# One inference step of a streaming encoder layer on one core: a later product with the values, an earlier weight split, low parts and copies on other engines

## The chip, the core and the metric

The kernel runs on 1 core of one Trainium2 chip. The engines of a core run side by side, each working through its own instructions in the order of the program, and they wait for each other at semaphores. In the profile they are called PE (TensorE: matrix products and transposes), PEld (the loading of PE's weights), DVE (VectorE), ACT (ScalarE), POOL (GpSimd) and SP (SyncE, which here issues most of the DMAs; "SPq" marks a DMA that it issues). The metric is the device time of one execution in microseconds (us). Products read SBUF and write PSUM; POOL works on SBUF alone.

## The reference: what is computed

One layer of a two-branch attention block, in float32, for a prompt of 1024 new positions and for a sample of 64 positions that has 512 cached positions behind it. Each of the two goes through the same steps, cut down here:

```python
h = rms_norm(x, norm_w) @ w_in          # 1024 -> 6144 columns
sb_q, sb_k, sb_v, sb_z, cb_q, cb_k, cb_v, cb_z, g_sb, g_cb = split(h)
# branch A ("sb"), 8 heads of 64: stick-breaking attention
z = sb_q @ sb_k.T * 0.125
w = where(s < t, exp(log_sigmoid(z) + sum of log_sigmoid(-z) over s < j < t), 0)
o_sb = w @ sb_v
# branch B ("cb"), 8 heads of 64: softmax over a band of the last 8 chunks of 64 and the own one,
# q and k normalised per head, with a learned bias by relative position
o_cb = softmax(cb_q @ cb_k.T * 0.125 + bias) @ cb_v
b_sb = (o_sb * silu(sb_z)) @ w_proj_sb
b_cb = (o_cb * silu(cb_z)) @ w_proj_cb
y = x + (sigmoid(g_sb) * b_sb + sigmoid(g_cb) * b_cb) @ w_out
```

The outputs are `y` for prompt and sample, and the new keys and values of both branches.

## The kernel before

**Split numbers.** A float32 factor of the large projections is held as two parts: the high part is a rounded copy (made by ACT), the low part is the rest (the factor less its high part, made by DVE or POOL). Three products, high times high, high times low and low times high, are summed in PSUM. So each block of weights, when it has landed in `wraw`, is "split": `W.split` (line 127) issues a copy on ACT (`whi`, line 117) and a subtraction (`wlo`, line 124) on POOL, or on DVE if that is passed as the engine. Both have two buffers.

**Stages.** First come the projections of all columns (lines 453 to 697, up to some 523 us), whose results go to DRAM. Then comes attention (547 to some 822 us): branch A, then branch B, each in four pairs of heads, each pair with the sample's block first (t = 8, both heads in one block of 128 rows) and then eight blocks of 128 prompt positions for each of its two heads, 17 blocks for a pair. Last come branch A's output projection (`proj_sb`), branch B's (`proj_cb`, line 967) and the output matrix (line 1509).

**Attention step by step.** The loop at line 1262 goes through the 136 blocks in the order of `seq`; in step i it issues the work of several blocks at different stages:
- `qk(i)`: PE's scores of block i into `z` (three PSUM buffers); for branch A ACT turns them into sigmoids `be` (line 1100), for branch B DVE adds the bias (line 1102).
- `mid(i-1)` for branch A: DVE's scan over `be` (line 1119). For branch B `soft(i-1)` takes the exponential on ACT (line 1110), and `mid(i-2)` a reciprocal on DVE (line 1121) and a scaling on ACT (line 1122).
- `tr(i-4)`: PE transposes the block's weights, in groups of up to four 128 x 128 blocks, into `pt` (two PSUM buffers, line 1150); a copy takes each group to `wT` in SBUF, on ACT (line 1159) for branch A and every fourth of branch B, else on DVE (line 1161). The last 64 rows of the sample's block are a group of their own (line 1155).
- `av(...)`: when both heads of two blocks (or the sample's block) are transposed, the product of values and `wT` is due two steps later: `avq` holds it with its step. It goes to `o`, which has a single PSUM buffer, and DVE multiplies it with the gate (line 1198 or 1200); POOL then issues its store to `d_osb` or `d_ocb`.
- `fill(n)`: n products of other work, taken from the generator `run_fill`, so that PE has something to do between. In a step with m of them, m // 2 come ahead of `av` and `tr`, the others behind. How many a step gets is written out by hand in `early` (line 1254): 11 for the very first block, 7 for each of the two after it, and a share by width of what is left.

**What the fill products are.** First four "units", blocks of 128 columns of the last projection: for each of three ranges of positions (`ci`) 24 products, 72 for a unit (line 842). Units 0 and 1 run ahead of attention, unit 2 within branch A from its first step on, and unit 3 from step 75 on. Within a unit, at the first product of `ci` 1 (line 849), the load of the block after next is issued and the next block is split (line 854; on DVE until step 75). Then follows `proj_sb`: 12 rounds of 24 products, after each 12 of which DVE multiplies the accumulator with a gate and writes it to SBUF (line 952). The accumulators (`acc`) have two PSUM buffers.

**The end of attention.** When the loop is done, 61 products of `proj_sb` are left. Line 1376 interleaves them with the preparation of branch B's output `o`: for each range of positions, `load_og` (line 899) issues four loads from `d_ocb` into `ot` (two buffers, each for two pairs of heads), then some fill products follow, then `make_og`: for each pair the high part on ACT (line 904) and the low part (line 909) on POOL for even pairs, on DVE for odd ones, and all on POOL in the second range. Loads of gates (`load_gcb`) and of the output matrix (`wsum`, line 1388) follow on SP, and then twelve rounds of `proj_cb`, with the split of their next weights on POOL every third round, and the sums of output weights (line 1399, 1401) and the low parts of kept columns (line 1018) also on POOL.

Of the kernel before, what the change touches and what calls it, by code (L numbers as in the profile page):

```python
# [32 lines left out]
def hybrid_step_kernel(ctx: ExitStack, tc: tile.TileContext, x_prompt, x_sample, c_sbk, c_sbv, c_cbk, c_cbv,  # L33
# [3 lines left out]
    V, A, G, TE, SP = nc.vector, nc.scalar, nc.gpsimd, nc.tensor, nc.sync  # L37
# [105 lines left out]
    def xk(s, k):  # L143
        return xhl[s][k // 4][:, k % 4]
# [9 lines left out]
    units = [("ev_act", 5120 + 128 * j, (AF.Copy, d_g["cb"][j])) for j in range(4, KT)]  # L154
# [392 lines left out]
    with ExitStack() as ph:  # L547
# [104 lines left out]
        for i in range(len(pairs)):  # L652
            bank, s1, u2, u3 = {}, {}, {}, {}
            for s in range(7):
                n = 7 * i + s
# [179 lines left out]
    def run_fill():  # L835
        for j, (kind, c, args) in enumerate(units):
            wh, wl = W.sp.pop(("u", j))
            for ci, (a, b) in enumerate(CH):
                ps = psF.tile([128, 512], F32, name="acc")
                for k in range(KT):  # L840
                    for n, (w, x) in enumerate(((wh, 0), (wh, 1), (wl, 0))):
                        TE.matmul(ps[:, :b - a], w[:, k], xk(x, k)[:, a:b], start=k == 0 and n == 0,  # L842
                                  stop=k == KT - 1 and n == 2)
                        if ci == k == n == 0 and j + 1 == len(units):
                            load_og("sb", 0, late["y"])
                            late["tbx"] = ExitStack()
                            late["tbp"] = late["tbx"].enter_context(tc.tile_pool(name="tbp", bufs=1, side="right"))
                            load_gate(late["tbp"], "gt", 0, d_g["sb"][0:2], 0)
                        if ci == 1 and k == 0 and n == 0:
                            if j + 2 < len(units):  # L850
                                load_unit(j + 2)
                            else:
                                load_proj(j + 2 - len(units))
                            W.split(("u", j + 1) if j + 1 < len(units) else ("p", 0), None if "sb" in late else V)
                        if k == KT - 1 and n == 2:
                            KIND[kind](*args, ci, a, b, ps)
                            if ci == 2:
                                prog[0] = j
                            if j + 1 == len(units):
                                ogq.extend((f, ci, p) for p in range(NPAIR) for f in (og_hi, og_lo))  # L860
                        yield 1
                        og_step(n == 0)
        late["tbt"] = xpool.tile([128, KT, T], F32, name="xm")
        for i, v in enumerate(proj_sb(late["tbp"])):
            yield v
            og_step(i % 3 == 2)
# [3 lines left out]
    def og(b, s, p):  # L870
        return xhl[s][s][:, p] if b == "sb" else late["og"][s][:, p]
# [4 lines left out]
    def load_proj(i):  # L876
        if i < 8:
            w = w_proj_sb if i < 4 else w_proj_cb
            c = (i % 4) * 256
            if i < 4:  # L880
                W.load(("p", i), wpool, w[:, c:c + 256].rearrange("(k p) n -> p k n", p=128), [128, 4, 256])
                return
            raw = wpool.tile([128, 4, 256], F32, name="wraw")
            for g in range(2):
                n = 512 * g + 128 * (i - 4)
                SP.dma_start(raw[:, :, 128 * g:128 * g + 128], w[:, n:n + 128].rearrange("(k p) n -> p k n", p=128))
            W.raw["p", i] = (raw, wpool, [128, 4, 256], "")
# [18 lines left out]
    def og_lo(b, ci, p):  # L906
        a, e = CH[ci]
        ot = ots.pop((ci, p))
        (V if p % 2 and (b, ci) != ("cb", 1) else G).tensor_tensor(out=og(b, 1, p)[:, a:e], in0=ot[:, :e - a],
                                          in1=og(b, 0, p)[:, a:e].bitcast(F32), op=OP.subtract)  # L910

    def make_og(b, ci):
# [6 lines left out]
    def load_gate(pool, name, key, us, ci):  # L919
        a, e = CH[ci]  # L920
        gts[key] = pool.tile([128, 2, 384], F32, name=name, bufs=2)
        for w, d in enumerate(us):
            SP.dma_start(gts[key][:, w, :e - a], d[:, a:e])
# [127 lines left out]
    def fill(n):  # L1051
        back = min(owed[0], 3)
        n += back
        owed[0] -= back
        while n > 0:
            if prog[0] == len(units) - 2 and "sb" not in late:
                owed[0] += n
                return
            v = next(gen, None)
            if not v:  # L1060
                return
            n -= 1
# [61 lines left out]
    def wbase(b, j):  # L1124
        return max(0, 2 * j - 4) if b == "cb" and j < 4 else 0

    flip = [0]

    def tr(i):
        b, p, t, hd = seq[i]  # L1130
        r = 128
        k0, n = band(b, t)
        be, _ = st.pop(i)
        j = t // 2 if t < 8 else 4
        q0 = (t % 2) * 128 if t < 8 else 0
        s0 = k0 - wbase(b, j)
        nblk = (n + 127) // 128
        groups = {}
        for kb in range(nblk):
            groups.setdefault((s0 + kb) // 4, []).append(kb)  # L1140
        for g, kbs in groups.items():
            wk = (b, p, j, hd, g)
            if wk not in wT:
                wT[wk] = ak.tile([128, 4, 256], F32, name="wT", bufs=6)
            w = wT[wk]
            pt = psT.tile([128, 4, 128], F32, name="pt")
            kr = 128
            for x, kb in enumerate(kbs):
                kr = min(128, n - kb * 128)
                TE.transpose(pt[:kr, x, :r], be[:r, kb * 128:kb * 128 + kr], ident[:r, :r])  # L1150
            m = len(kbs)
            sl = (s0 + kbs[0]) % 4
            if kr < 128:
                m -= 1
                A.activation(w[:kr, sl + m, q0:q0 + r], pt[:kr, m, :r], AF.Copy)
            if m:
                flip[0] += 1
                if b == "sb" or flip[0] % 4 == 0:
                    A.activation(w[:, sl:sl + m, q0:q0 + r], pt[:, :m, :r], AF.Copy)  # L1159
                else:  # L1160
                    V.tensor_copy(w[:, sl:sl + m, q0:q0 + r], pt[:, :m, :r])
# [99 lines left out]
    avq = []  # L1261
    for i in range(len(seq) + LAG + 2):
        m = 0
        if i < len(seq):
            b, p, t, hd = seq[i]
            if b == "cb" and p == 0 and t == 8 and hd == 0:
                sbx.close()
                yst = ExitStack()
                late["y"] = yst.enter_context(tc.tile_pool(name="ay", bufs=2))
            if (b, p, t, hd) == ("sb", 3, 6, 0):  # L1270
                load_bias(0)
                load_bias(1)
        if 0 < i <= len(seq) and seq[i - 1][0] == "cb":
            soft(i - 1)
        if 1 < i <= len(seq) + 1 and seq[i - 2][0] == "cb":
            mid(i - 2)
        if i < len(seq):
            qk(i)
            if hd == 0:
                if t % 2 == 1 or t == 8 and (b, p) != ("sb", 0):  # L1280
                    load_z(b, p, t // 2 if t < 8 else 4)
                prefetch(b, p, t)
            acc += amount[b] * wt[b](band(b, t)[1]) / tot[b]
            acc += early.get((b, p, t, hd), 0)
            m = int(acc) - emitted
            emitted += m
        else:
            m = 8
        if 0 < i <= len(seq) and seq[i - 1][0] == "sb":
            mid(i - 1)  # L1290
        flush()
        if i == len(seq) // 2 + LAG + 3:
            late["sb"] = True
        fill(m // 2)
        while avq and avq[0][0] <= i:
            av(*avq.pop(0)[1:])
        if 0 <= i - LAG < len(seq):
            tr(i - LAG)
            b, p, t, hd = seq[i - LAG]
            if t == 8 or hd == 1 and t % 2 == 1:  # L1300
                avq.append((i + 2, b, p, t // 2 if t < 8 else 4))
        fill(m - m // 2)
    flush(True)
    yst.close()
# [71 lines left out]
    for ci in range(3):  # L1376
        if ci < 2:
            load_og("cb", ci, late["y"])
        fill((22, 24, 100000)[ci])
        if ci == 2:  # L1380
            load_gcb(0)
            load_og("cb", ci, late["y"])
            load_gcb(1)
            late["h"][1] = [xpool.tile([128, 4, T], F32R, name=f"x{s}") for s in "ab"]
            sig(0)
        make_og("cb", ci)
# [95 lines left out]
    for i in range(2):  # L1482
# [3 lines left out]
        for q, s in enumerate(OP_):  # L1486
            n = 8 * i + q
# [13 lines left out]
            for c in range(2) if s != "b" else ():  # L1501
# [9 lines left out]
                p = ps[:]  # L1511
# [15 lines left out]
                if s in (3, 4, 5, 6):  # L1527
# [4 lines left out]
                    if s == 4:  # L1532
                        p, x = u3[c], xrs.pop((i, 1, 1, c))
# [61 lines left out]
```

## Time and profile before

| | us |
|---|---|
| Median of 3 runs (lowest to highest) | 972.03 (970.86 to 972.68) |
| The profiled execution's own time | 971.06 |
| Its span, first to last instruction | 969.3 |
| PE busy | 951.8 (98%) |
| PEld busy | 906.1 (93%) |
| DVE busy | 587.9 (61%) |
| ACT busy | 475.5 (49%) |
| POOL busy | 393.6 (41%) |

The granted clock of TensorE was 1.000 throughout. Rows of a timeline give the start and the duration in us, the engine, the line, the operation, what is written and read, the shapes, the count of merged instructions, and in brackets the engine's idle time before with what ended it. A list of waits gives who waited for what: us in total, how many times, the longest. Rows of the DMA view give, last, the median time from issue to landing. Ends of PE's products are modelled, so that neighbouring ones overlap in the rows.

### The profile page before, as it was taken

How to read it: one execution, taken by the hardware profiler on the slowest of the kernel's cores; microseconds unless marked ns; L12 is line 12 of the kernel's file. 1: busy time of each engine (PE TensorE's matmuls, PEld its weight loads, DVE VectorE, ACT ScalarE, POOL GpSimd, SP SyncE). 2: the span in 40 equal slices, each digit the busy share in tenths (PEclk: the TensorE clock that was granted, in tenths of full speed). 3: DMA queues.
4: the chain of work that ended last, by engine and by line, in shares of the span. 5: the costliest groups of instructions: out<-in, count | busy, mean ns of one | idle time of the engine just before them, and what ended most of it. 6: DMA issues, size and time to landing. Idle time of an engine off the chain costs nothing.

```text
span 969.3 us, 20419 instructions
## 1 busy us (share of the span) xinstructions
PE 951.8 (98%) x7604; PEld 906.1 (93%) x7604; DVE 587.9 (61%) x1166; ACT 475.5 (49%) x1056; POOL 393.6 (41%) x391
## 2 busy tenths in 40 slices
PE   6999999999999999999999999999999999999998
PEld 5999999999999999999999987777888988999998
DVE  5456665696454555543332298776777865499735
ACT  6544443344444343333332377667886874465220
POOL 3276664215454566655542200011331111586641
PEclk9999999999999999999999999999999999999999
DMA  7727567534646565555533997769799832862742
GB/s 243 226 84 244 196 223 253 177 93 133 183 138 191 182 182 176 154 178 168 164 96 92 271 251 216 181 173 246 226 292 255 245 105 82 260 193 70 221 133 78
DMA packets 173512, 176.28 MB, mean 182 GB/s; under 512 B 30753, under 2 KB 157597, under 8 KB 173286
## 3 DMA queue, kind: packets, MB, share of 16 engines
q1 hardware_dynamic: 161878, 159.98, 56.2%
q10 hardware_dynamic: 8720, 8.33, 2.7%
q0 software_dynamic: 2816, 6.69, 2.2%
q8 instruction: 60, 0.98, 0.5%
q14 instruction: 38, 0.31, 0.1%
HBM read 112.94 MB, written 62.00 MB: 180 GB/s over the span
## 4 chain that ended last, share of the span: by engine, by line
PE 95%; ACT 1%; DMA 1%; SPq 1%; issue 0%; POOL 0%; DVE 0%; ACTq 0%; DVEq 0%
PE b L673 30%; PE acc L467 20%; PE b L1509 8%; PE z L1097 7%; PE o L1189 7%; PE pt L1150 7%; PE b L990 5%; PE acc L842 5%; PE acc L948 4%; PE pk L352 1%; DMA wrawx<-in_w_in_dram 1%; PE pt L280 1%; PE acc L1545 1%; DMA ot<-d_ocb 0%; PE acc L598 0%
## 5 line engine op out<-in xcount | busy, mean ns | idle before, releaser
L1150 PE MATMUL pt<-ident,be 128*128 128x128 f32 (+1 forms) x568 | 87.7, 278 | 1.9 <-ACT wT L1159 1.6
L1097 PE MATMUL z<-ks,sq 128*128 128x320 f32 (+5 forms) x384 | 88.3, 338 | 0.0
L1119 DVE TENSOR_TENSOR_SCAN be<-be,imp 128x128 f32<-128x128 f32 (+7 forms) x64 | 83.2, 1340 | 7.6 <-ACT be L1100 7.6
L1150 PEld LDWEIGHTS pt<-ident,be 128*128 128x128 f32 (+1 forms) x568 | 66.3, 140 | 15.2 <-issue 4.6
L1159 ACT ACTIVATE wT<-pt 128x512 f32<-128x512 f32 (+3 forms) x125 | 58.1, 500 | 44.6 <-PE pt L1150 44.5
L467 PE MATMUL acc<-whi,xa 128*128 128x256 f32 x256 | 74.2, 292 | 0.0
L467 PE MATMUL acc<-wlox,xm 128*128 128x256 f32 x256 | 70.7, 278 | 0.0
L467 PE MATMUL acc<-whi,xm 128*128 128x256 f32 x256 | 70.7, 278 | 0.0
L467 PE MATMUL acc<-wlo,xa 128*128 128x256 f32 x256 | 70.7, 278 | 0.0
L467 PE MATMUL acc<-whix,xb 128*128 128x256 f32 x256 | 70.6, 278 | 0.0
L467 PE MATMUL acc<-whix,xm 128*128 128x256 f32 x256 | 70.6, 278 | 0.0
L681 DVE TENSOR_TENSOR u<-b,s 128x256 f32<-128x256 f32 (+1 forms) x56 | 24.2, 439 | 73.2 <-PE b L673 72.1
L1097 PEld LDWEIGHTS z<-ks,sq 128*128 128x128 f32 x384 | 63.9, 190 | 2.0 <-ACT be L1100 0.9
L1189 PE MATMUL o<-wT,vp 128*64 128x256 f32 (+1 forms) x608 | 64.2, 356 | 0.0
L1189 PEld LDWEIGHTS o<-wT,vp 128*64 128x64 f32 x608 | 40.3, 136 | 23.6 <-issue 6.6
L1122 ACT ACTIVATE be<-be,sm 128x640 f32<-128x640 f32 (+5 forms) x68 | 47.3, 695 | 17.0 <-DVE sm L1121 17.0
L124 POOL TENSOR_TENSOR wlo<-wraw,whi 128x1024 fp32r<-128x1024 f32 x15 | 36.4, 2427 | 46.7 <-ACT whi L117 43.2
L746 POOL DMA_DIRECT2D d_osb<-zt x20 | 10.8, 540 | 104.5 <-DVE zt L1198 72.2
L1100 ACT ACTIVATE be<-z 128x384 f32<-128x384 f32 (+6 forms) x104 | 48.1, 519 | 4.5 <-PE z L1097 3.9
L437 POOL TENSOR_TENSOR whix<-ws,whix 128x512 fp32r<-128x512 f32 x28 | 36.9, 1317 | 31.6 <-ACT whix L436 31.6
L1110 ACT ACTIVATE be<-be,sm 128x640 f32<-128x640 f32 (+5 forms) x68 | 47.3, 696 | 4.7 <-DVE sm L1102 4.3
L467 PEld LDWEIGHTS acc<-whi,xa 128*128 128x128 f32 x256 | 47.9, 188 | 0.1
(306 smaller groups left out, 3184.3 us busy)
## 6 DMA issues: line engine op xcount, KB each, us to landing
wraw<-in_w_in_dram SPq DMA_DIRECT2D x31, 512.0 KB, 4.4
wrawx<-in_w_in_dram SPq DMA_DIRECT2D x17, 512.0 KB, 4.5
sq<-d_qsbT SPq DMA_DIRECT2D x32, 192.0 KB, 4.2
sq<-d_qcbT SPq DMA_DIRECT2D x32, 192.0 KB, 5.3
xt<-in_x_prompt_dram SPq DMA_DIRECT2D x8, 512.0 KB, 5.2
d_kcbT<-hl SPq DMA_DIRECT2D x8, 512.0 KB, 4.4
d_qcbT<-hl SPq DMA_DIRECT2D x8, 512.0 KB, 3.1
d_ksbT<-hl SPq DMA_DIRECT2D x16, 256.0 KB, 2.8
```

The source lines that it names most:

```text
L467: TE.matmul(ps, x, w, start=m == 0, stop=m == len(steps) - 1)
L673: TE.matmul(ps[:, :m], w[:, hl_, k], right[s](x)[:, k, a:b], start=s < 3 and k == 0 and e == 0, stop=k == 3 and e == 2, skip_group_check=s ...
L842: TE.matmul(ps[:, :b - a], w[:, k], xk(x, k)[:, a:b], start=k == 0 and n == 0, stop=k == KT - 1 and n == 2)
L990: TE.matmul(pp[uu][:, :n], w[:, p, uu * 128:uu * 128 + 128], g[:, a:e], start=p == 0 and m == 0, stop=p == NPAIR - 1 and m == 2)
L1097: TE.matmul(z[:, :m], s[:, e, q0:q0 + 128], ks[:, h, o + x:o + y], start=(e, h) == parts[0], stop=(e, h) == parts[-1])
L1100: A.activation(be[:r, x:y], z[:r, :m], AF.Sigmoid, scale=-0.125)
L1110: A.activation(be[:, :n], be[:, :n], AF.Exp, bias=kp[:, j:j + 1], scale=-1.0, accum_out=kp[:, 2:3])
L1119: V.tensor_tensor_scan(be[:r, n - 1::-1], be[:r, n - 1::-1], im[:, ::-1], 0.0, op0=OP.mult, op1=OP.max)
L1150: TE.transpose(pt[:kr, x, :r], be[:r, kb * 128:kb * 128 + kr], ident[:r, :r])
L1159: A.activation(w[:, sl:sl + m, q0:q0 + r], pt[:, :m, :r], AF.Copy)
L1189: TE.matmul(o[hd * 64:hd * 64 + 64, c0:c1], vv[:kr, kb, hd * 64:hd * 64 + 64], wT[b, p, j, hd, s // 4][:kr, s % 4, c0:c1] if j < 4 else wT ...
L1509: TE.matmul(ps[:, t], left[s](xs_, k)[:, ts_], wt_[:, k], start=s < 3 and t == k == e == 0, stop=k == 3 and e == 2, skip_group_check=s > 2 ...
```

## The change

It has four places. In the fill generator the split moves out of the `if` of the load and gets its own place: for unit 3's weights (issued while unit 2 runs) it is the first product of the fourth k of `ci` 0, product 9 of the unit instead of product 24; for all others it stays. The load stays where it was. In `og_lo` the first range of branch B joins the second: all four low parts on POOL. In `tr` the copies of the second group of the last branch A blocks (pair 3, t = 7, two heads) go to DVE instead of ACT. The sample's product with the values is due three steps after its transposes instead of two, in all eight pairs of heads. And the first of the three fills at the end of attention takes 26 products instead of 22.

```diff
@@ -851,6 +851,7 @@
                                 load_unit(j + 2)
                             else:
                                 load_proj(j + 2 - len(units))
+                        if (ci, k, n) == ((0, 3, 0) if j + 2 == len(units) else (1, 0, 0)):
                             W.split(("u", j + 1) if j + 1 < len(units) else ("p", 0), None if "sb" in late else V)
@@ -906,7 +907,7 @@
     def og_lo(b, ci, p):
         a, e = CH[ci]
         ot = ots.pop((ci, p))
-        (V if p % 2 and (b, ci) != ("cb", 1) else G).tensor_tensor(out=og(b, 1, p)[:, a:e], in0=ot[:, :e - a],
+        (V if p % 2 and (b, ci) not in (("cb", 0), ("cb", 1)) else G).tensor_tensor(out=og(b, 1, p)[:, a:e], in0=ot[:, :e - a],
                                           in1=og(b, 0, p)[:, a:e].bitcast(F32), op=OP.subtract)
@@ -1155,7 +1156,7 @@
             if m:
                 flip[0] += 1
-                if b == "sb" or flip[0] % 4 == 0:
+                if b == "sb" and not (p == 3 and t == 7 and g == 1) or b == "cb" and flip[0] % 4 == 0:
                     A.activation(w[:, sl:sl + m, q0:q0 + r], pt[:, :m, :r], AF.Copy)
                 else:
                     V.tensor_copy(w[:, sl:sl + m, q0:q0 + r], pt[:, :m, :r])
@@ -1298,7 +1299,7 @@
             if t == 8 or hd == 1 and t % 2 == 1:
-                avq.append((i + 2, b, p, t // 2 if t < 8 else 4))
+                avq.append((i + (3 if t == 8 else 2), b, p, t // 2 if t < 8 else 4))
@@ -1376,7 +1377,7 @@
         if ci < 2:
             load_og("cb", ci, late["y"])
-        fill((22, 24, 100000)[ci])
+        fill((26, 24, 100000)[ci])
```

## The prediction

> **What bounds the kernel now.** I read the page first, then TensorE's (PE's) waits, then the timeline at each of them, then the queues that feed them.
>
> ```profile
> span 969.3 us, 20419 instructions
> PE 951.8 (98%) x7604; PEld 906.1 (93%) x7604; DVE 587.9 (61%) x1166; ACT 475.5 (49%) x1056; POOL 393.6 (41%) x391
> ```
>
> PE is busy for 98% of the span. The change alters none of its products, so it can only win PE's idle time, 17.5 us, or add to it. The list of PE's waits says where that is:
>
> ```profile
> PE pt L280 <- DVE xn L269: 8.0, 2, 7.4
> PE pt L1150 <- ACT wT L1159: 1.6, 2, 1.1
> PE acc L948 <- DVE xm L952: 1.4, 1, 1.4
> ```
>
> The 8.0 us are the start, which the diff doesn't touch. What it can touch are three stalls, 3.05 us together, which PE's timeline places:
>
> ```profile
> 555.83 0.33 PE L1150 MATMUL pt<-ident,be 128*128 128x128 f32 x1 [1.06 <-ACT wT L1159]
> 674.11 0.79 PE L1150 MATMUL pt<-ident,be 128*128 128x128 f32 x5 [0.58 <-ACT wT L1159]
> 830.53 0.42 PE L948 MATMUL acc<-xa,whi 128*128 128x320 f32 x1 [1.41 <-DVE xm L952]
> ```
>
> Each part of the change meets one of them. So for each: does its stall go, and what is late next?
>
> **Part 1, the split of unit 3's weights 15 fill products sooner (L854).** Rows of PE, ACT, DVE and SyncE's queue, and of the DMA view for 540 to 556 us:
>
> ```profile
> 548.56 1.92 PE acc L842 x11
> 553.70 0.71 PE L1150 MATMUL pt<-ident,be 128*128 128x128 f32 x5
> 548.20 0.81 ACT L1100 ACTIVATE be<-z 128x288 f32<-128x288 f32 x2 [0.45 <-PE z L1097]
> 553.69 1.05 ACT L117 ACTIVATE whi<-wraw 128x1024 fp32r<-128x1024 f32 x1
> 555.16 0.61 ACT L1159 ACTIVATE wT<-pt 128x512 f32<-128x512 f32 x1
> 549.10 1.36 DVE L1119 TENSOR_TENSOR_SCAN be<-be,ims 128x576 f32<-128x576 f32 x1 [1.29 <-ACT be L1100]
> 554.77 1.23 DVE L124 TENSOR_TENSOR wlo<-wraw,whi 128x1024 fp32r<-128x1024 f32 x1 [3.35 <-ACT whi L117]
> 543.54 0.44 SPq L111 DMA_DIRECT2D wraw<-in_w_in_dram  x1
> wraw<-in_w_in_dram SPq DMA_DIRECT2D x1, 512.0 KB, 8.2
> ```
>
> Now the 1.05 us copy at 553.69 stands ahead of the copy of the sample block's weights (555.16), for whose PSUM buffer PE waits. Without it that copy could start when the block's first four transposes are done, at about 554.4, end by 555.0, and release PE at 555.1: a gain of 0.74.
>
> But where does it go? Unit 2's products 0 to 10 are issued in the sample block's own step (the x11 row; `early` gives that step 11). Product 9, the new place, is thus behind that block's two sigmoids (done 549.01) and ahead of its scan. The block's weights were asked for at 543.54 and took 8.2 us: they land at 551.7. So ACT, in order, waits there from 549.01 to 551.8; the copy ends at 552.9. DVE, in order too, does the low part next, to 554.1, and only then the scan that ran at 549.10: 1.36 us, to 555.45. PE's five transposes, at 553.70 now, start at 555.5; the fourth ends by 556.1, ACT's 0.61 us copy by 556.75, and the transpose that ran at 555.83 runs at about 556.8. That is 1.0 later than now, not 0.74 sooner. Queued behind ACT's wait are the sigmoids of the next two blocks; they come at 553.0 and 553.3, when nobody needs them yet. Bounds: -0.74 if the load is there, +1.8 if the whole delay of the transposes stays. I take +1.0, since the 8.2 us are this very load's row.
>
> By the Trainium skill (SBUF — State Buffer, § The DMA setup-cost knee) a DMA takes some 2 us and its bytes at 436 GB/s, an estimate of 3.2 us for these 512 KB. By it the weights would be there at 546.7, the split would cost nothing at its new place, and the sum below would be 1.74 lower; the trace's 8.2 us disagrees, with the DMA engines shared by other loads.
>
> **Part 2, the sample's product with the values a step later (L1301).**
>
> ```profile
> 555.91 0.59 PE L1097 MATMUL z<-ks,sq 128*128 128x384 f32 x2
> 556.43 0.95 PE L1189 MATMUL o<-wT,vs 128*64 128x64 f32 x20
> 585.67 0.61 DVE L1198 SCALAR_TENSOR_TENSOR zt<-o,vl,zt 128x128 f32<-128x128 f32 x2 [3.14 <-PE o L1189]
> 585.63 0.60 PE L1097 MATMUL z<-ks,sq 128*128 128x384 f32 x2
> 586.38 0.95 PE L1189 MATMUL o<-wT,vs 128*64 128x64 f32 x20
> 678.65 0.60 PE L1097 MATMUL z<-ks,sq 128*128 128x384 f32 x2
> 679.39 0.95 PE L1189 MATMUL o<-wT,vs 128*64 128x64 f32 x20
> ```
>
> In the first pair nothing comes before it, and the product starts 0.07 before the modelled end of the scores (556.50). In the next four pairs (first and last shown) it starts 0.15 after that end: the one PSUM buffer `o` is still read by DVE (to 586.28) for the block before. That is 0.21 too late, four times: 0.86. One step later DVE is done, and scores and a transpose stand between. In the last three pairs fill products stand between already: nothing. The buffers that it holds a step longer (weights six deep, gates four deep) come round only later steps. DVE's read of it also moves a step, behind one more scan: no cost. I take -0.86; ends 0 and -0.86.
>
> **Part 3, two copies of the last stick-breaking block to DVE (L1158).**
>
> ```profile
> 672.15 1.15 PE L1150 MATMUL pt<-ident,be 128*128 128x128 f32 x8
> 673.05 0.49 PE L1097 MATMUL z<-ks,sq 128*128 128x256 f32 x2
> 671.50 1.09 ACT L1159 ACTIVATE wT<-pt 128x512 f32<-128x512 f32 x2
> 673.46 1.09 ACT L1159 ACTIVATE wT<-pt 128x512 f32<-128x512 f32 x2
> 674.81 0.69 DVE L1161 COPY wT<-pt 128x512 f32<-128x512 f32 x1 [0.80 <-PE pt L1150]
> ```
>
> PE waits at 674.11 for the first copy of 673.46. ACT loses half of the pair at 671.50, 0.5, and so comes to it at 673.05: PE goes on at 673.7, a gain of 0.4. It can't be more than 0.58, as PE has scores until 673.54. DVE takes two copies of 0.69, at 671.9 and 673.3; behind them wait a reciprocal and ACT's scaling by it, which then starts at 672.75 in place of 673.17, still in time. -0.4, ends 0 and -0.58.
>
> **Part 4, all low parts of branch B's first chunk on POOL (L909), with fill 26 for 22 (L1379).**
>
> ```profile
> 827.29 2.29 POOL L909 TENSOR_TENSOR og<-ot,og 128x384 fp32r<-128x384 f32 x2 [1.71 <-DMA ot<-d_ocb]
> 827.83 2.17 DVE L909 TENSOR_TENSOR og<-ot,og 128x384 fp32r<-128x384 f32 x2 [2.31 <-DMA gt<-d_gsb]
> 829.93 1.01 DVE L952 TENSOR_TENSOR xm<-acc,gt 128x384 f32<-128x384 f32 x2
> 828.80 2.06 SPq L899 DMA_DIRECT2D ot<-d_ocb  x4
> 834.00 1.99 POOL L909 TENSOR_TENSOR og<-ot,og 128x384 fp32r<-128x384 f32 x2 [0.15 <-ACT og L904]
> 837.87 0.38 SPq L1388 DMA_DIRECT2D wo<-in_w_out_dram  x1
> 845.64 2.40 POOL L1399 TENSOR_TENSOR wo<-wo,wo 128x1024 f32<-128x1024 f32 x1 [5.92 <-DMA wo<-in_w_out_dram]
> 854.17 2.86 POOL L124 TENSOR_TENSOR wlo<-wraw,whi 128x1024 fp32r<-128x1024 f32 x1
> 858.18 0.34 PE L990 MATMUL b<-og,wlo 128*128 128x384 f32 x1
> ```
>
> DVE's 2.17 us hold up the multiplication (829.93) that frees PE's accumulator. Without them it runs when PE's products end, at 827.2, and PE goes straight on: 1.41 idle and a restart, 1.6. Fill 26 puts that multiplication ahead of the low parts in DVE's order as well; alone it would win the same, beside part 4 nothing, and it moves no DMA.
>
> What is late next: POOL needs 1.0 for each of four parts (1.99 for two), so the second pair's buffer is free at 831.2, where DVE freed it at 830.0. The reload queued for it on SyncE goes 1.2 later, and with it chunk 1's low parts (834.00), chunk 2's reload, and the loads of the output weights (837.87), behind which POOL's sum at 845.64 waits. From there POOL works without a gap through the low part at 854.17, which ends at 857.03. PE uses it at 858.18 (its weight load some 0.17 sooner): 0.98 to spare now. So of the 1.6 there stay 0.98 less s, the delay of those loads. s lies between 0 (the loads catch up) and 1.2. I take 0.6, as they wait in part for DMA bandwidth. Net -0.4; ends -0.98 and +0.2, and -1.6 if POOL's chain should speed up.
>
> **Sum.** +1.0 - 0.86 - 0.4 - 0.4 = -0.66 against the profiled execution's 971.06 (its span and 1.76 around it): 970.4. That execution lies 0.97 below the median of the three runs, 972.03, so I forecast 971.4 for the median: no change that can be measured. The three runs differ by 1.8 among themselves; 0.2%, 1.94 us, is about what a measurement can tell here.
>
> **Rivals.**
> A, faster, as the weights are there: the page of the profile gives 4.4 us as the median of 31 such loads:
>
> ```profile
> wraw<-in_w_in_dram SPq DMA_DIRECT2D x31, 512.0 KB, 4.4
> ```
>
> With that they land at 547.9, before the sigmoids end, and part 1 gives -0.74: sum -2.4, 969.6. Against it: the load's own row, and its order in SyncE's queue is unchanged. Chance 0.14.
>
> B, faster, as POOL's later chain is no bound: part 4 keeps its 1.6, sum -1.86, 970.2, at the bound. Against it: POOL's rows stand gapless from 845.64 on. Chance 0.10.
>
> C, slower, as the weights land still later: each us of landing after 551.7 is a us on ACT, DVE's scan and PE. From 552.4 on the sum is above zero; at 554.3 it is +1.94. Its price at 10.8 us from issue to landing is +1.94, 974.0; at 12, 975.2. For it: the DMA engines are 9 to 10 tenths busy there. Against it: 8.2 was measured for it. Chance 0.14.
>
> D, the change moves the waits and nothing else, my forecast: chance 0.62, its own range 969.9 to 972.9 by the ends of parts 2 to 4 and the runs' spread.
>
> Range: from 969.2, a little under A, to 973.4, between D's end and C. Faster by over 0.2%: A 0.14, half of B 0.05 and D's low tail 0.03, so 0.22. Slower: C, 0.14. Within: 0.64.
>
> **What will show it.** Part 1: ACT's copy L117 in that step starts near 551.8 after some 2.8 us idle released by the weights' DMA, the sample's scan follows L124 on DVE, and PE has a wait of about 1.8 ahead of the five transposes in place of the 1.06; A would show L117 at 549 and no such wait. Part 2: the sample's product no longer starts after the scores' end. Part 3: 0.1 to 0.2 in place of 0.58. Part 4: no wait at L948, four L909 in a row on POOL, and a new wait of some 1 us at L990 released by POOL's L124. If PE's idle time falls by more than 2 us, my step on the landing or that on POOL's chain is wrong.

## The result, and the profile after

| | before | after |
|---|---|---|
| Median of 12 runs, us (lowest to highest) | 972.18 (970.86 to 974.33) | 968.79 (967.3 to 972.29) |
| The profiled execution's own time | 971.06 | 968.7 |
| Its span | 969.3 | 966.9 |

The ratio of the times is 0.9966, with a 95% interval from 0.9955 to 0.9977: the change made the kernel 3.3 us faster, 2.2 to 4.4 by the interval. The forecast was 971.4, with a range down to 969.2 and 0.7 us to gain. A second measurement of the same kernel, below, gave 0.9976 (0.9964 to 0.9988), 2.3 us. Both gains are larger than the one I forecast; they differ between them by about a us, and 2.3 us alone would still have been inside the forecast's range, whose low end is 2.8 us below 972.03. So the size of the miss is uncertain by that much, and which terms were wrong has to be read from the profiles.

From the page of the kernel after, the span and the busy times, and behind them the list of PE's waits (us in total, times, longest):

```profile
span 966.9 us, 20406 instructions
PE 950.5 (98%) x7604; PEld 905.5 (94%) x7604; DVE 587.1 (61%) x1166; ACT 475.9 (49%) x1054; POOL 396.5 (41%) x393
```

```profile
PE pt L280 <- DVE xn L269: 8.5, 2, 7.4
PE acc L467 <- ACT whi L117: 2.1, 1, 2.1
PE pt L1151 <- DVE be L1120: 0.8, 1, 0.8
PE pt L1151 <- ACT wT L1160: 0.4, 2, 0.2
```

Lines behind the new `if` are one higher than before. The wait at L949 (L948 before) is gone, and no wait at L991 (L990 before) has come in its place. The two waits of L1151 for ACT, 1.6 before, are 0.4, and a wait of 0.8 for DVE's scan is new. At the start (L280, L467) this execution waited about 1 us longer than before's; no edit reaches there.

To see where the time went I set each product of PE against the same product of before's profile; the difference of their starts is PE's **shift** at that place. Four landmarks of the kernel after, whose partners in the profile of before stand in the prediction at 555.83, 585.63, 678.65 and 858.18, and then the rows behind each part:

```profile
556.58 0.33 PE L1151 MATMUL pt<-ident,be 128*128 128x128 f32 x1 [0.22 <-ACT wT L1160]
586.28 0.60 PE L1098 MATMUL z<-ks,sq 128*128 128x384 f32 x2
678.12 0.59 PE L1098 MATMUL z<-ks,sq 128*128 128x384 f32 x2
855.81 0.34 PE L991 MATMUL b<-og,wlo 128*128 128x384 f32 x1
...
543.58 0.38 SPq L111 DMA_DIRECT2D wraw<-in_w_in_dram  x1
551.59 1.06 ACT L117 ACTIVATE whi<-wraw 128x1024 fp32r<-128x1024 f32 x1 [1.98 <-DMA wraw<-in_w_in_dram]
552.68 1.23 DVE L124 TENSOR_TENSOR wlo<-wraw,whi 128x1024 fp32r<-128x1024 f32 x1 [4.28 <-ACT whi L117]
553.83 1.35 DVE L1120 TENSOR_TENSOR_SCAN be<-be,ims 128x576 f32<-128x576 f32 x1
555.23 0.77 PE L1151 MATMUL pt<-ident,be 128*128 128x128 f32 x5 [0.78 <-DVE be L1120]
...
587.39 0.95 PE L1190 MATMUL o<-wT,vs 128*64 128x64 f32 x20
673.60 0.77 PE L1151 MATMUL pt<-ident,be 128*128 128x128 f32 x5 [0.16 <-ACT wT L1160]
...
818.07 0.80 SPq L924 DMA_DIRECT2D gt<-d_gsb  x2
825.79 3.95 POOL L910 TENSOR_TENSOR og<-ot,og 128x384 fp32r<-128x384 f32 x4 [0.90 <-DMA ot<-d_ocb]
836.62 1.48 SPq L1389 DMA_DIRECT2D wo<-in_w_out_dram  x3
844.15 2.40 POOL L1400 TENSOR_TENSOR wo<-wo,wo 128x1024 f32<-128x1024 f32 x1 [5.42 <-DMA wo<-in_w_out_dram]
852.69 2.86 POOL L124 TENSOR_TENSOR wlo<-wraw,whi 128x1024 fp32r<-128x1024 f32 x1
850.91 2.37 DVE L1036 TENSOR_TENSOR acc<-xm 128x512 f32<-128x512 f32 x2
```

The shift is +0.59 just before Part 1 (the longer start, partly made up since). From there on ("given back" is what PE loses again later of the gain at L949):

| part | forecast | kernel after's profile | how |
|---|---|---|---|
| 1 | +1.0 | +0.04 | shift 545 to 565: +0.59 to +0.63 |
| 2 and 3 | -0.86 - 0.4 | -1.36 | 565 to 690: +0.63 to -0.73 |
| 4, at L949 | -1.6 | -1.67 | 820 to 840: -0.70 to -2.37 |
| 4, given back | +1.2 | 0.00 | 840 to the end |
| between the parts | | +0.03 | 690 to 820 |
| sum | -0.66 | -2.96 | |

With the +0.59 ahead of them these make the spans' 2.4. The row of Part 1 holds some 0.1 that Part 2 costs in the same stretch: the shift grows by 0.09 and 0.10 there in the two kernels below that have Part 2 without Part 1. So the sizes of Parts 2 and 3 and of the stall at L949 were right, and two terms account for the miss: Part 1's cost, and what POOL's chain gives back.

### The profile page after: what moved, and what is told of

The parts are those of the page before. It is cut to its first block, busy times and chain, and to the rows that moved or that the text cites. A ratio compares the mean times of both kernels' runs of the same rounds, so it can differ in the third digit from the quotient of the medians.

```text
span 966.9 us, 20406 instructions
## 1 busy us (share of the span) xinstructions
PE 950.5 (98%) x7604; PEld 905.5 (94%) x7604; DVE 587.1 (61%) x1166; ACT 475.9 (49%) x1054; POOL 396.5 (41%) x393
## 4 chain that ended last, share of the span: by engine, by line
PE 94%; DMA 2%; ACT 1%; SPq 1%; DVE 1%; POOL 0%; issue 0%; ACTq 0%
PE b L673 30%; PE acc L467 20%; PE b L1510 8%; PE o L1190 7%; PE pt L1151 7%; PE z L1098 7%; PE acc L949 5%; PE b L991 5%; PE acc L842 2%; PE pk L352 1%; DMA wrawx<-in_w_in_dram 1%; DMA wraw<-in_w_in_dram 1%; DMA ks<-d_ksbT 1%; PE pt L280 1%; PE acc L1546 1%; SPq L51 0%
## 5 line engine op out<-in xcount | busy, mean ns | idle before, releaser
L1151 PE MATMUL pt<-ident,be 128*128 128x128 f32 (+1 forms) x568 | 87.7, 278 | 1.5 <-DVE be L1120 0.8
L1151 PEld LDWEIGHTS pt<-ident,be 128*128 128x128 f32 (+1 forms) x568 | 65.7, 140 | 14.2 <-issue 4.6
L467 PE MATMUL acc<-whi,xa 128*128 128x256 f32 x256 | 74.2, 292 | 0.0
L467 PE MATMUL acc<-wlox,xm 128*128 128x256 f32 x256 | 70.8, 278 | 0.0
L467 PE MATMUL acc<-whi,xm 128*128 128x256 f32 x256 | 70.8, 278 | 0.0
L467 PE MATMUL acc<-wlo,xa 128*128 128x256 f32 x256 | 70.7, 278 | 0.0
L467 PE MATMUL acc<-whix,xb 128*128 128x256 f32 x256 | 70.6, 278 | 0.0
L467 PE MATMUL acc<-whix,xm 128*128 128x256 f32 x256 | 70.6, 278 | 0.0
L467 PEld LDWEIGHTS acc<-whi,xa 128*128 128x128 f32 x256 | 47.9, 188 | 0.1
```

The source lines that it names most:

```text
L467: TE.matmul(ps, x, w, start=m == 0, stop=m == len(steps) - 1)
```

## Experiments

The profile of an experiment is one execution. Its shifts are read against the same profile of before as above; they resolve some hundredths of a us, where a time resolves about one. Each ratio is to runs of the kernel before that were measured beside it; these had medians of 971.31 to 972.86, so it is the ratios that can be compared between groups of experiments, not the medians.

**Part 1 alone, and the change without it.** The first is the kernel before with only the line of the split's own place (cut out here), the second the kernel after with product 24 again in that line:

```diff
+if (ci, k, n) == ((0, 3, 0) if j + 2 == len(units) else (1, 0, 0)):
```

```diff
-if (ci, k, n) == ((0, 3, 0) if j + 2 == len(units) else (1, 0, 0)):
+if (ci, k, n) == (1, 0, 0):
```

> The kernel before with the earlier split of unit 3's weights (part 1) alone. Theory M (the profile after read as it stands): the weights' landing is set by the DMA queue and not by PE, so the copy L117 starts at the landing, 551.3 to 551.8, PE's five transposes start at about 555 and the next one 0.8 to 1.0 after the one of before's profile (555.83) less however late PE itself is; PE's idle time ahead of it adds 1.0 to 1.9, against the 1.06 of before: time +0.0 to +0.8 us. The prediction: +1.0, at most +1.8. Rival A (weights there at 549): no idle ahead of the transposes, -0.74.

> The kernel after with unit 3's weights split at fill product 24 again (parts 2, 3 and 4 without part 1). Theory M (part 1 is worth 0.0 to +0.8): the same as the kernel after or up to 0.8 faster, 968.0 to 969.0 where the kernel after has 968.8; the wait of 1.06 ahead of the transpose is back and that of before the five transposes is gone. The prediction (part 1 costs 1.0): 967.8. If part 1 gained 0.74 after all (rival A): 969.5.

Measured: alone 971.21, ratio 0.9994 (0.9984 to 1.0005); without it 969.42, 0.9980 (0.9970 to 0.9989). No cost of a us can be seen in either. In the profile of Part 1 alone the weights landed at 551.29 with PE's shift at +0.30, and the part cost 0.17.

**The weights there sooner, or split later.** The kernel after, with the load of unit 3 issued 12 fill products sooner, or with the split at product 18:

```diff
-if ci == 1 and k == 0 and n == 0:      # the load
+if (ci, k, n) == ((0, 4, 0) if j == 1 else (1, 0, 0)):
```

```diff
-if (ci, k, n) == ((0, 3, 0) if j + 2 == len(units) else (1, 0, 0)):
+if (ci, k, n) == ((0, 6, 0) if j + 2 == len(units) else (1, 0, 0)):
```

> The kernel after with unit 3's load issued 12 fill products sooner, ahead of the loads of the values and gates in SyncE's order. Theory M (each us that the weights land later is a us on the five transposes, down to the point where the weights are there when the sigmoids end): the load is issued at 538 to 539 and lands at 545 to 548, ACT's L117 runs at 549.1 without a wait, and the wait ahead of the transposes goes: -0.7 against the kernel after, 968.1, unless the values that were moved behind it are late for their first product at 556. Rival (the queue only shares the engines otherwise): it lands at 551 as before, and the time is the kernel after's 968.8.

> The kernel after with unit 3's weights split at fill product 18 (first of the block two after the sample's) in place of 9: after the sample block's scan in DVE's order, and after the landing. Theory M: ACT's copy L117 runs at about 552.5 without a wait for the landing, DVE's scan of the sample runs at 549 again, the wait of 0.8 ahead of the five transposes is gone; ACT's two sigmoids at 554.6 and 554.9 still stand ahead of the weights' copy, so the wait ahead of the next transpose is 0.2 to 0.5 in place of before's 1.06: 0.5 to 0.8 less than the kernel after, 968.0 to 968.3. The prediction's account would give the same place -0.74 against +1.0 at product 9: 967.1. Rival: nothing there matters, the same as the kernel after.

Measured: 969.25, 0.9958 (0.9946 to 0.9970), and 969.07, 0.9965 (0.9952 to 0.9978). With the load sooner ACT no longer waits:

```profile
538.48 0.40 SPq L111 DMA_DIRECT2D wraw<-in_w_in_dram  x1
549.12 1.05 ACT L117 ACTIVATE whi<-wraw 128x1024 fp32r<-128x1024 f32 x1
```

Part 1 then gains 0.95, and at product 18 it gains 0.98. Neither kernel is shown to be faster than the kernel after, though; in their profiles 1.50 and 2.86 are lost again behind 865, which the last experiments take up. All profiles with the split at product 9 that wait for the landing lie on one line, to about 0.1, if the landing is taken less PE's shift ahead of it:

| landing less shift | 549.91 | 550.31 | 550.72 | 550.91 | 550.91 | 550.99 |
|---|---|---|---|---|---|---|
| Part 1, us | -0.95 | -0.57 | -0.17 | +0.03 | +0.04 | +0.17 |
| kernel (labels below) | after_sum5 | fill_123 | low_halves | after_again | after | p1_alone |

A us of landing is a us on PE, as the prediction had it, and 551.79, the landing in before's profile, gives +0.9 on that line. But that landing was the latest of all 13 profiles in which the load was issued at its old place; their median is 550.64, and there the part gains 0.2. The bound of -0.74 was too near as well: it is -0.95.

**Part 2 alone.**

```diff
-avq.append((i + 2, b, p, t // 2 if t < 8 else 4))
+avq.append((i + (3 if t == 8 else 2), b, p, t // 2 if t < 8 else 4))
```

> The kernel before with the sample's product with the values one step later (part 2) alone. Theory M: in four steps (near 586, 616, 646 and 679 us) PE gains 0.2 to 0.3 each, -1.1 in all, and nothing else moves by over 0.1: time -1.1. The prediction: -0.86. Rival: the total of the change's gain is here, because a later product also takes a wait off PE that the table of waits does not list, -2 or more.

Measured: 970.10, ratio 0.9984 (0.9975 to 0.9992). In its profile the shift falls by 0.28, 0.31, 0.31 and 0.20 at the four pairs, 1.10 together. Of this 0.23 is lost again at 672, just ahead of the stall that Part 3 is for, so that 0.83 to 0.84 is left between 565 and 690; and ahead of that 0.10 is lost at the first pair, for which I had nothing. Together with Part 3 the fall between 565 and 690 is 1.3 to 1.4 in every kernel that has both, so Part 3 is worth about 0.5; at its own stall the shift falls by 0.43 in the kernel after. The forecasts of 0.86 and 0.4 held as totals. What else made this kernel faster is in the waits of the two kernels that leave Part 4's code as it was, Part 1 alone first:

```profile
PE acc L949 <- DVE xm L953: 0.8, 1, 0.8
```

```profile
PE acc L948 <- DVE xm L952: 0.3, 1, 0.3
```

The wait of 1.41 on which Part 4's gain was built was 0.8 and 0.3 in these executions. It is set by when branch B's first outputs land, for which the low parts wait: with PE's shift taken off, DVE began them at 827.83 in before, 827.11 with Part 1 alone and 826.57 with Part 2 alone. In before's profile they came late.

**Part 4 alone, and each half of it.** The kernel before with both edits (`p4_alone`), with the first line only, and with the second only:

```diff
-(V if p % 2 and (b, ci) != ("cb", 1) else G)
+(V if p % 2 and (b, ci) not in (("cb", 0), ("cb", 1)) else G)
-fill((22, 24, 100000)[ci])
+fill((26, 24, 100000)[ci])
```

> The kernel before with the low parts of branch B's first chunk on POOL and fill 26 for 22 (part 4) alone. Theory M: the wait of 1.41 at L948 goes, PE gains 1.65, and POOL's low part L124 of the weights p6 ends 0 to 0.4 ahead of its use by PE, without a wait of PE: -1.65. The prediction: POOL's chain comes 0.6 later and gives 1.2 back, a wait of about 1 us of PE ahead of the first product with those weights, -0.4. M+ (the landing of the first outputs decides: if the first low part starts as late as before's 827.3, the chain ends 0.2 to 1.2 too late, if it starts 0.8 sooner it does not): between the two, and the profile shows which.

> The kernel before with the low parts of branch B's first chunk all on POOL, fill 22 kept. Theory M: as part 4 as a whole: no wait at L948; what is given back, is given back between 884 and 905 at L1509, and only in an execution in which DVE's second L1035 runs into POOL's low part of p6 (it takes 2.9 in place of 1.5): 0 or 1.5. The prediction: a wait of about 1 at L990 for POOL's low part of p6.

> The kernel before with fill 26 for 22 and nothing else (DVE keeps its low parts). The prediction: it wins the whole 1.6 at L948, since the multiplication stands ahead of the low parts in DVE's order; DVE's low parts come some 1.0 later than now. Theory M: the same, with the reloads for the next chunk issued up to 1 us later than in part 4 as a whole, and the loads of the output weights with them. Rival (it is only the order on POOL that matters): the wait at L948 stays.

Measured: 970.92, ratio 0.9987 (0.9978 to 0.9997); the halves, one run each, 974.47 and 971.19 (in both, PE had fallen 1.6 us behind between 300 and 520 already, evenly, where no edit is). All three gain 1.67 at L948. With the fill alone it stays. With both edits 1.60 of it is lost again between 865 and 935, and with the low parts alone 0.83 at L990 (a wait for DVE's low part of the weights p5; `p4` to `p7` are `proj_cb`'s four blocks of weights) and 2.25 behind 865. So there is a give-back, but mostly at another place than the prediction's, and not in each execution. What the losing ones have in common, in the profile of both edits:

```profile
852.90 3.60 DVE L1035 TENSOR_TENSOR acc<-xm 128x512 f32<-128x512 f32 x2
853.09 2.85 POOL L124 TENSOR_TENSOR wlo<-wraw,whi 128x1024 fp32r<-128x1024 f32 x1
886.26 0.39 PE L1509 MATMUL b<-wlo,xa 128*128 128x256 f32 x1 [0.36 <-POOL wlo L1372]
```

DVE's pair of subtractions takes 3.60 in place of before's 2.35, as the second of them stands still until POOL's low part of p6 has ended. From there DVE, ACT and POOL are late together, and PE waits at L1509 for the next stage's weights. The view of the chain that ended last shows it for 845 to 893: in the kernel after (first row) it stays on PE, while with both edits alone (the next two) it runs over DVE from the pair on.

```profile
845.00 34.30 PE b L991 x209
...
844.87 8.16 PE b L990 x47
853.06 3.44 DVE acc L1035 x2
```

**The same kernel again, and three ways to take the two apart.** The kernel after unchanged; with POOL's low part of p6 in two instructions; with DVE and POOL sharing the first chunk's low parts again (fill 26 kept); and this with the sooner load:

```diff
-(eng or G).tensor_tensor(out=l, in0=raw, in1=h[:].bitcast(F32), op=OP.subtract)
+for c in ((slice(0, 2), slice(2, 4)) if key == ("p", 6) else (slice(0, shape[1]),)):
+    (eng or G).tensor_tensor(out=l[:, c], in0=raw[:, c], in1=h[:, c].bitcast(F32), op=OP.subtract)
```

```diff
-(V if p % 2 and (b, ci) not in (("cb", 0), ("cb", 1)) else G)
+(V if p % 2 and (b, ci) != ("cb", 1) else G)
```

> The kernel after once more, unchanged, beside the next three on the same chip. Theory L (DVE's L1036, with two inputs in SBUF, and POOL's low part L124 of p6 take turns; where the second L1036 falls behind L124 it takes 2.9 in place of 1.5, and with part 4's later loads DVE's chain is then past its slack of some 1.6 us and PE loses 1.5 to 2.9 between 880 and 925): the profile shows either 1.5 there and no loss behind 880, or 2.9 and a loss of 1.5 to 2.9; median 968.8. The account by which part 4 keeps its gain in every execution: no loss behind 880, whatever the duration of L1036.

> The kernel after with POOL's low part L124 of the weights p6 done in two instructions of 512 columns in place of one of 1024. Theory L: DVE waits for one half at most, so the second L1036 takes at most 1.9 (0.56 of its own work behind what is left of 1.2), DVE's chain is 1.0 less late in the executions that lose, and the loss behind 880 is 0.5 us or less: median 967.8 to 968.5, and few runs above 969.5. Rival (lateness comes from the loads alone, the lock only moves slack): the same as the kernel after, with its runs up to 972; the extra instruction costs POOL 0.1 or less.

> The kernel after with the low parts of branch B's first chunk on DVE and POOL in turn again, as in the kernel before, fill 26 kept (parts 1, 2, 3 and half of part 4). Theory L: the wait at L949 is gone all the same (the multiplication stands ahead of the low parts on DVE), the loads of the output weights and gates keep up with PE, so DVE's chain has its slack in both cases and nothing is lost behind 880: median 967.5 to 968.3, 0.5 to 1.3 less than the kernel after, with a narrower spread. The prediction's account (either half alone wins the same, POOL's chain gives back only with the low parts there): the same direction, 1.2 less. Rival: the same as the kernel after within 0.3.

> The kernel of the run before this (fill 26, low parts shared) with unit 3's load 12 fill products sooner as well. If the sooner load is worth the 0.8 us that the profile of that change alone showed between 545 and 560, and nothing is given back behind 880: 0.7 less again, 966.8 to 967.6, the fastest of all. Rival: the sooner load only moves PE ahead of the loads of the later branch, and the gain is given back at 880 to 925: the same as the run before this.

| | median | ratio (interval) | lowest to highest |
|---|---|---|---|
| after_again, 12 runs | 968.89 | 0.9976 (0.9964 to 0.9988) | 966.98 to 971.37 |
| low_halves, 5 runs | 968.37 | 0.9970 (0.9958 to 0.9982) | 968.04 to 969.20 |
| fill_123, 5 runs | 968.17 | 0.9967 (0.9955 to 0.9979) | 967.73 to 968.70 |
| fill_123_load, 7 runs | 968.77 | 0.9973 (0.9962 to 0.9983) | 968.07 to 970.33 |

The intervals overlap; none is shown to be faster than the kernel after. In `after_again` the second subtraction took 1.52 and nothing was lost behind 865, as in the kernel after. In `low_halves` the profiled execution was not one of those in which the pair is held up by the low part of p6 (it took 2.16), so it decided nothing. But the last two show the prediction's own wait, that of PE for POOL's low part of p6: 0.2 us in `fill_123`, and 0.64 in `fill_123_load`:

```profile
852.85 2.84 POOL L124 TENSOR_TENSOR wlo<-wraw,whi 128x1024 fp32r<-128x1024 f32 x1
855.75 0.44 PE L991 MATMUL b<-og,wlo 128*128 128x384 f32 x1 [0.64 <-POOL wlo L124]
```

Their loss between 840 and 865 is 0.50 and 1.22. It follows from the prediction's 0.98 to spare: POOL's low part ends, with PE's shift taken off, at 858.52 and 859.24; PE needs it at 858.01 (857.03 + 0.98). In the kernel after it ends at 857.92, so 0.09 was left.

**POOL's second sum out of the chain.** The sum of output weights ahead of the low part of p6 is done in round 5: in the kernel after; in `fill_123_load`; and there with the two halves.

```diff
-        if j == 2:
+        if j == 5:
             G.tensor_tensor(out=wsum[2], in0=wsum[3], in1=wsum[2], op=OP.subtract)
```

> The kernel after with POOL's second sum of output weights (L1402, 2.4 us) done in round 5 in place of round 2, so that it no longer stands ahead of the low part L124 of p6. Theory P (POOL's chain bounds part 4): L124 starts 1 to 2 us sooner in relation to PE, when ACT's copy of p6 is done; it then stands at or ahead of DVE's first L1036 and the second is not held for 2.9; no wait at L991 and no loss behind 880: median 967.8 to 968.5, few runs above 969.5. Rival (the sum is not the cause, DVE's chain is late by the gates' loads): runs up to 972 as with the kernel after, median 968.9. Rival (lock): DVE's first L1036 is held behind L124 for 2 us or more, and the loss behind 880 is there in every execution: 970.

> The kernel with unit 3's load sooner, fill 26 and shared low parts, in whose profile PE waited 0.6 (0.9 lost) for POOL's low part of p6, with the second sum moved to round 5. Theory P: that wait is gone, PE is 3.5 us ahead of the kernel before's profile from 830 to the end: 0.9 to 1.2 faster than without the move, median 967.6 to 967.9. Rival (something else holds PE there, or the loads of the last stage do): the same 968.8 as without the move.

> The kernel of the run before this with POOL's low part of p6 in two instructions of 512 columns. Lock theory: where DVE's L1036 has to wait for POOL it waits 1.2 at most in place of 2.4, so the slow executions come nearer: median the same within 0.4, highest run lower by 0.5 to 1. Rival: no difference.

Measured: `after_sum5` 969.83, ratio 0.9982 (0.9973 to 0.9991), runs from 968.97 to 970.42; `best_sum5` 969.11, 0.9974 (0.9963 to 0.9984); `best_halves` 967.75, 0.9960 (0.9947 to 0.9974). The first was no faster, against what I expected, and its profile shows what its lock rival said; that it is slower than the kernel after is not shown, as the intervals overlap. The second is no faster than `fill_123_load` (0.9973), as its rival said. The first kernel, and then the third:

```profile
850.86 2.40 POOL L124 TENSOR_TENSOR wlo<-wraw,whi 128x1024 fp32r<-128x1024 f32 x1 [1.35 <-ACT whi L117]
851.37 3.60 DVE L1036 TENSOR_TENSOR acc<-xm 128x512 f32<-128x512 f32 x2
884.73 0.39 PE L1510 MATMUL b<-wlo,xa 128*128 128x256 f32 x1 [0.41 <-POOL wlo L1373]
```

```profile
849.86 2.99 POOL L125 TENSOR_TENSOR wlo<-wraw,whi 128x512 fp32r<-128x512 f32 x2 [0.52 <-ACT whi L117]
850.36 3.06 DVE L1037 TENSOR_TENSOR acc<-xm 128x512 f32<-128x512 f32 x2
```

No wait is left at L991, but the low part now meets DVE's subtractions, and 2.82 are lost behind 865. With the halves the pair takes 3.06 in place of 3.60 (3.65 in the second kernel's profile). Whether that made the third kernel 1.4 us faster than the second is not shown: in the profiled executions it lost 1.56 behind 865 and the second 0.80. It has the lowest median of all, though not the lowest ratio (0.9958, with the load sooner); its interval overlaps both of the kernel after, so that it beats that kernel is not shown.

Over all 17 profiles the loss behind 865 goes with one number, the end of DVE's pair with PE's shift taken off:

| end of the pair | 854.77 to 856.25 (9 profiles) | 856.76 | 857.55 | 857.96 | 858.15 | 858.79 | 858.87 | 858.87 |
|---|---|---|---|---|---|---|---|---|
| lost, 865 to 935 | 0.00 | 0.80 | 1.56 | 1.60 | 1.50 | 2.25 | 2.82 | 2.86 |
| kernel | | best_sum5 | best_halves | p4_alone | load_sooner | p4_pool_only | after_sum5 | split18 |

(The one that is left, `fill_123_load`, has 856.99 and no loss; it had already lost 1.22 at L991, which leaves 855.77.) Past about 856.1 it is a us for a us to within 0.6. Before's profile, at 854.77, had 1.3 to spare there; the kernel after's, at 855.66, had 0.4.

When the pair ends depends on its duration and on its start, and the start hangs on a landing too. In all 17 profiles ACT starts the sigmoid of the gates `ot` 0.5 to 0.6 us after the recorded landing of the first of their two loads, after a wait of 2.8 to 5.0, and DVE waits for ACT. In the kernel after, and then with both edits of Part 4 alone:

```profile
846.40 0.74 ACT L966 ACTIVATE ot<-ot 128x640 f32<-128x640 f32 x1 [3.94 <-DMA ot<-d_gcb]
847.18 0.83 DVE L996 TENSOR_TENSOR b<-b,ot 128x640 f32<-128x640 f32 x1 [2.42 <-ACT ot L966]
...
849.16 0.83 DVE L995 TENSOR_TENSOR b<-b,ot 128x640 f32<-128x640 f32 x1 [3.01 <-ACT ot L965]
```

With PE's shift taken off the pair began at 852.42 in before, at 853.28 in the kernel after, and at 853.1 to 855.3 in the seven that lost. With the kernel after's 2.37 for the pair six of these seven would still have ended past 856.1, at 856.4 to 857.6 (an estimate); the longer pair adds 0.7 to 1.8 to that. So late gates and the meeting with POOL share the loss, and no run takes the two apart.

## Why the prediction was wrong

**Part 1: the step that failed is "they land at 551.7".** The order of the waits was right: ACT behind the landing, DVE's low part, the scan, five transposes. From the landing to the transposes I had 3.8, and the kernel after has 3.7, by its row of the DMA view (543.58 + 7.9, to 555.23):

```profile
wraw<-in_w_in_dram SPq DMA_DIRECT2D x1, 512.0 KB, 7.9
```

But I took the landing from before's profile as a fixed number, and it keeps no fixed distance to PE: relative to PE it came at 550.91 in the kernel after, 0.88 sooner, and it ranged from 549.91 to 551.79 (with one at 548.35) over the 13 profiles. I had one execution, and it was the latest. Rival A, "the weights are there", was not what happened in any profile with the split at product 9 and the load in its old place, since ACT waited in all of them; but its gain came already with a landing at 549.91. Rival C's later landing came in none.

**Part 4: the step that failed is "I take 0.6", the delay s of POOL's loads.** Gain and spare were right: 1.67 against 1.6, and the two waits at L991 begin where 0.98 runs out. But s, POOL's low part against its end in before's profile with PE's shift at 820 taken off, was not +0.6: it is -0.78 in the kernel after (855.55 + 0.70 less 857.03). The four low parts in a row do take 3.95 as I had it; yet they began at 825.79, 0.8 sooner on PE's scale than before's 827.29, because SyncE issued the loads ahead of them faster. In before's profile two such issues took

```profile
818.77 2.11 SPq L923 DMA_DIRECT2D gt<-d_gsb  x2
```

where the kernel after's took 0.80; both begin at 818.77 on PE's scale, and only one of the other 15 profiles has the long issue, `p4_pool_only`. The edits reach none of it, and why an issue takes longer is not shown. That start is 0.8 of the 1.4 by which s was off. The other 0.6 is the delay of the loads that I had put in, and it did not come: POOL's sum, which waits for the output weights, began at 844.15, on the same scale again 0.8 sooner than before's 845.64. With only one of the two, some 0.5 to 0.7 would have been given back (an estimate: 1.67 less 0.98, and s at -0.2 or 0). My end "-1.6 if POOL's chain should speed up" is what the profile shows. Over the profiles with Part 4 and POOL's sum in its old place s is between -1.5 and +0.5, and in the two profiles of Part 4's old code -2.3 and -2.6: before's execution was late here too. So rival B's condition was met in the kernel after's profile, with 0.09 to spare.

**What the prediction did not see** is the second follower, DVE's L1035 behind POOL's low part. The Trainium skill has the rule (SBUF — State Buffer, § Who interferes with whom): a DVE instruction with two inputs in SBUF and a GpSimd instruction that reads SBUF share an interface, and the one that is issued second waits for the whole of the other. The traces agree: the second subtraction ends 0.56 after POOL's instruction in before (854.77 after 854.21) as in Part 4 alone (856.50 after 855.94); only which of POOL's instructions it meets differs, one of 1.0 or one of 2.4. Before's rows of the first case, DVE's pair and POOL's instruction of 1.0 that it meets:

```profile
852.42 2.35 DVE L1035 TENSOR_TENSOR acc<-xm 128x512 f32<-128x512 f32 x2
852.75 1.46 POOL L1018 TENSOR_TENSOR xb<-xm,xa 128x384 fp32r<-128x384 f32 x1
```

Together with the landing of the gates, which sets the pair's start, it decided on 0.8 to 2.9 us in seven profiles, and the forecast has no chance for it.

**Parts 2 and 3 were right**, -1.36 against -1.26, with the 0.16 that I had left over at 673.60. In Part 2's total there is some luck: alone it gained 1.10 at the four pairs where I had 0.86, and lost 0.33 at two places where I had nothing.

Both misses come from one error: two terms of the sum, +1.0 and +1.2, hung on when a DMA of one execution landed, and both were late ones. I also priced rivals A and B one at a time, 969.6 and 970.2; that both terms could fail in one run has no price and no chance in the forecast, though by its own numbers the two together are -3.6. By the median landing of the 13 profiles Part 1 is -0.2, and Part 4 has 0.6 to 1.7 to gain at L948 (1.67 in before's execution; 1.02 and 0.58 in the other two of Part 4's old code, which lost 0.65 and 1.09 less there), 1.1 in the mean: with Parts 2 and 3 a sum of -2.7 where nothing is given back, which lies within both measured intervals. With Part 4's low parts on POOL and the sum in its old place, four of eight profiles gave nothing back and four gave 1.5 to 3.1. What stays open: 7 of the 24 runs of the kernel after took over 970; that these are executions in which DVE met POOL's low part would fit the seven profiles that lost behind 865, but neither profile of that kernel shows it. Open as well is how much of that loss is the meeting itself and how much the late gates.

## What to carry to other kernels

A wait that ends with a DMA's landing is a draw, not a size: ask how PE and the landing move against each other, and give such a term the spread of several executions before it goes into a sum with a sign. When a stall goes, follow all chains that were hidden behind it, not only that with the least to spare in the one profile: here POOL's had 0.98 and DVE's 1.3, and DVE's lost more. And where DVE and POOL both read two operands from SBUF, look at which long POOL instruction a short DVE one on the path can fall behind.

## What the runs showed of the hardware

- DVE and POOL stand still for each other instruction by instruction. DVE's pair of 128x512 subtractions took 2.1 to 2.4 where it met POOL's 1.0 us instruction and 3.6 to 4.1 where it met the low part of 2.4 in one piece; POOL's own 1.02 us instruction took 1.46 to 1.54 in the first case, and the low part 2.84 to 2.86 where a subtraction stood ahead of it.
- Which of the two happens depends on some tenths of a us. With the sum in its old place the pair began 0.03 to 0.35 ahead of POOL's instruction of 1.0 where it took 2.1 to 2.4, and 0.3 to 0.9 behind it where it took 3.6 to 4.1. Part 1 alone and Part 2 alone had the long pair too (4.0), and lost nothing, as PE was less far ahead.
- The load of 512 KB took 7.2 to 8.2 us from issue to landing over 13 executions of the same stage.
- Taking 2.4 us out of POOL's chain ahead of the low part did not make the kernel faster (ratio 0.9982, where the kernel after had 0.9966 and 0.9976): in the profile it brought that instruction in front of DVE's pair.
